# Six PSUM banks in turn and twelve pairs of weight buffers in the output stage of a hybrid decoder layer

## Chip, cores and metric

One NeuronCore of one Trainium2 chip runs the whole kernel. The metric is the device time of one execution in microseconds (us): the median of 3 runs before the change is 2421.57 us, the lowest 2419.29 and the highest 2424.53.

## What is computed

One decoder layer over 2048 tokens of width 1024, in float32, with 16 learned meta tokens in front. One input projection of 8712 columns feeds two branches: sliding-window attention (16 heads, 4 key heads, window 128, sinks) and an mLSTM (4 heads, chunked). Then the two branches are projected, merged and projected again:

```python
def _hybrid_mixer(u, w_in, ...):
    proj = u @ w_in
    (a_q, a_k, a_v, a_z, m_qk, m_v, m_i, m_f, m_o, m_z, g_a, g_m) = jnp.split(proj, SPLIT_POINTS, axis=-1)
    att = _swa_sink_branch(...)
    y_a = (att * jax.nn.silu(a_z)) @ w_attn_out
    cell = _mlstm_cell(...)
    hm = _head_layernorm(o_gate * cell, head_norm)
    y_m = (hm * jax.nn.silu(m_z)) @ w_mlstm_out
    merged = jax.nn.sigmoid(g_a) * y_a + jax.nn.sigmoid(g_m) * y_m
    return merged @ w_out
...
    h = h + _rmsnorm(y, norm_post[layer])
```

The change touches the last lines: the three matrix products with `w_attn_out`, `w_mlstm_out` and `w_out`, each 1024 by 1024, over 2048 tokens.

## The kernel before

Every product of two float32 matrices is made of three products of split operands: each operand is written as a high part in the format float32r and a low part that holds the rest, and high by high, high by low and low by high are summed in one PSUM bank. A *pair* of weight buffers is a high tile (`whi`) and a low tile (`wlo`) of 128 by 512 numbers; a *unit* (`un`) is the same for the data.

The program has two stages. The **projection stage** runs over two halves of the tokens, and in each over 18 blocks of weight columns; the work of attention and mLSTM is cut into small steps that are slipped between the projection matmuls. It leaves the attention result, the mLSTM result and the gates in DRAM (`att_d`, `hm_d`, `gate_d`). The **output stage** (the loop over `s` that ends the kernel) runs over four passes of 512 tokens. A pass has three products of two weight blocks each: attention (call its blocks A0 and A1, `ph` 0, L929), mLSTM (B0 and B1, `ph` 1, L929) and the last projection (O0 and O1, L951). A block has four groups of 24 matmuls of 128x512; a group fills one PSUM bank, and VectorE (DVE) reads it out: L934 in A0 and A1, L936 and L937 in B0 and B1 (which also splits the merged tile into a unit, L889 on ScalarE (ACT) and L890 on DVE), and L959 or L967 in O0 and O1 after ACT has squared it (L956).

`load_w` (L163) brings a block of weights: eight tiles of raw weights by DMA on SyncE's queue (L175, three buffers in the output stage, and two more in the projection stage), each split by ACT (`whi`, L181) and DVE (`wlo`, L182). The pairs come from the pool `wp`; in the output stage the first two of a block's eight come from tiles of their own (`whi2`, `wlo2`, four of each), so that a block takes six pairs of `wp` there and eight in the projection stage.

The order of TensorE (PE) is the order of the program text (`manual_schedule`). The order of the other engines' instructions and of the DMA issues is made ahead of the run by the framework's scheduler, which takes the earliest in the program among those that it holds ready; the raw loads and the splits are moved ahead by the priorities `DMA_LEAD` and `SPLIT_LEAD` (30 and 2; 100 for the second block of all). Each engine then works through its list strictly in order. A tile that is asked of a pool waits until the oldest of the pool's buffers under that name has been read for the last time.

PSUM's eight banks belong to four pools: `ps_p` (2, name `pj`), `ps_s` (one tile of 2 banks), `ps_t` (2, `tr`) and `ps_a` (2, `acc`). In the output stage only the two of `ps_p` are used.

Of the kernel before, what the change touches and what calls it, by code (L numbers as in the profile page):

```python
# [9 lines left out]
F32 = mybir.dt.float32  # L10
# [13 lines left out]
SB = 512  # L24
# [66 lines left out]
def hybrid_layer(ctx: ExitStack, tc: tile.TileContext, x, xT, mx, mxT, gpre, w_all, w2, negs, cw, cb,  # L91
                 gbias, hnorm, gpost, rope, ident, sel, bmask, out):
    nc = tc.nc
# [3 lines left out]
    def pool(name, bufs=1, space=None, es=ctx):  # L97
        kw = {} if space is None else {"space": space}
        return es.enter_context(tc.tile_pool(name=name, bufs=bufs, **kw))
# [1 line left out]
    const = pool("const")  # L101
    dram = pool("dram", 1, DRAM)
    units = pool("units", 16)
    wp = pool("wp", 9)
    stage = pool("stage", 4)
    ps_p = pool("ps_p", 2, PSUM)
    ps_s = pool("ps_s", 1, PSUM)
    ps_t = pool("ps_t", 2, PSUM)
    ps_a = pool("ps_a", 2, PSUM)
# [4 lines left out]
    def f(t):  # L114
        return t.bitcast(F32)
# [89 lines left out]
    with ExitStack() as es1:  # L205
# [490 lines left out]
        def token_proj(us, o, wh, wl, w, ps=None):  # L696
            if ps is None:
                ps = ps_p.tile([128, SB], F32, name="pj")
            n = 0
            for k in range(KT):  # L700
                for a, ww in ((0, wh), (0, wl), (1, wh)):
                    T.matmul(ps[:, :w], lhsT=us[k][:, a, o:o + 128], rhs=ww[k][:, :w],  # L702
                             start=(n == 0), stop=(n == 3 * KT - 1))
                    n += 1
                    if n % SLOT == 0 and n < 3 * KT:
                        slot()
            return ps

        def feat_proj(us, i, wh, wl):
            ps = ps_p.tile([128, SB], F32, name="pj")  # L710
            n = 0
            for k in range(KT):
                for a, ww in ((0, wh), (1, wh), (0, wl)):
                    T.matmul(ps, lhsT=ww[k][:, 128 * i:128 * i + 128], rhs=us[k][:, a],  # L714
                             start=(n == 0), stop=(n == 3 * KT - 1))
                    n += 1
                    if n % SLOT == 0 and n < 3 * KT:
                        slot()
            return ps
# [32 lines left out]
        for c in range(NHALF):  # L752
# [7 lines left out]
            for pi, (kind, arg, cols) in enumerate(PLAN):  # L760
# [24 lines left out]
                if kind == "A":  # L785
                    chains = []
                    for i in range(HALF_BLOCKS):
                        rs = None
                        if c == 0 and arg == 0:
# [9 lines left out]
                            if i < 4:  # L799
                                ps = first_ps[i]  # L800
                            else:
                                ps = token_proj(u[1], (i % 4) * 128, wh, wl, w, first_ps[i] if i < 6 else None)
# [3 lines left out]
                        else:  # L806
                            ps = token_proj(u[i // 4], (i % 4) * 128, wh, wl, w)
# [34 lines left out]
                elif kind == "M":  # L842
                    for i in range(HALF_BLOCKS):
                        mrep = max_rows(c, i + nb - HALF_BLOCKS, arg)
                        ps = token_proj(u[i // 4], (i % 4) * 128, wh, wl, w)
# [6 lines left out]
                else:  # L852
# [9 lines left out]
                    for n, (i, s) in enumerate(order):  # L862
                        nm, ix = arg[i]
                        ps = feat_proj(u[s], i, wh, wl)
# [19 lines left out]
    gpost_t = p2.tile([128, D], F32, name="gpost", bufs=1)  # L884
    nc.sync.dma_start(out=gpost_t, in_=gpost.partition_broadcast(128))

    def split_unit(src):
        un = units.tile([128, 2, SB], R, name="un")
        S.copy(un[:, 0], src)  # L889
        tt(un[:, 1], src, f(un)[:, 0], ALU.subtract)  # L890
        return un

    for s in range(SEQ // SB):
        sl = slice(s * SB, (s + 1) * SB)
        part = [None] * KT
        mg = [None] * KT
        for ph, (src, zn, gn) in enumerate(((att_d, "az", "ga"), (hm_d, "mz", "gm"))):
            us = []
            with (tc.high_priority(offset=150) if s == 0 and ph == 0 else ExitStack()):
                for k in range(KT):  # L900
                    early = s == 0 and ph == 0
                    if early:
                        a = p2.tile([128, SB], F32, name=f"part{k}", bufs=1)
                    else:
                        a = stage.tile([128, SB], F32, name="xs")
                    nc.sync.dma_start(out=a, in_=src[k, :, sl])
                    if early:
                        if k % 2 == 0:
                            zz = p2.tile([128, D], F32, name="y", bufs=4)
                        z = zz[:, k % 2 * SB:(k % 2 + 1) * SB]  # L910
                    else:
                        z = p2.tile([128, SB], F32, name="zl", bufs=3)
                    nc.sync.dma_start(out=z, in_=gate_d[zn][k, :, sl])
                    if ph == 0:
                        tt(a, a, z, ALU.mult)
                    else:
                        stt(a, a, hn_t[:, k:k + 1], z, ALU.mult, ALU.mult)
                    us.append(split_unit(a))
            for nb_ in range(2):
                wh, wl = load_w(w2, (2 * ph + nb_) * D * SB, SB, p2)  # L920
                for i in range(4):
                    j = nb_ * 4 + i
                    th = p2.tile([128, SB], F32, name="tl", bufs=3)
                    nc.sync.dma_start(out=th, in_=gate_d[gn][j, :, sl])
                    ps = ps_p.tile([128, SB], F32, name="pj")
                    n = 0
                    for k in range(KT):
                        for a, ww in ((0, wh), (1, wh), (0, wl)):
                            T.matmul(ps, lhsT=ww[k][:, 128 * i:128 * i + 128], rhs=us[k][:, a],  # L929
                                     start=(n == 0), stop=(n == 3 * KT - 1))  # L930
                            n += 1
                    if ph == 0:
                        part[j] = p2.tile([128, SB], F32, name=f"part{j}", bufs=1)
                        stt(part[j], th, 1.0, ps, ALU.add, ALU.mult)  # L934
                    else:
                        stt(th, th, 1.0, ps, ALU.add, ALU.mult)  # L936
                        tt(part[j], part[j], th, ALU.add)  # L937
                        mg[j] = split_unit(part[j])
        w_o = load_w(w2, 4 * D * SB, SB, p2)
        ys, sss = [], []  # L940
        for i in range(4):
            ys.append(p2.tile([128, D], F32, name="y", bufs=4))
            sss.append(p2.tile([128, 4], F32, name="yss", bufs=4))
        for nb_ in range(2):
            wh, wl = w_o if nb_ == 0 else load_w(w2, 5 * D * SB, SB, p2)
            for i in range(4):
                ps = ps_p.tile([128, SB], F32, name="pj")
                n = 0
                for k in range(KT):
                    for a, ww in ((0, wh), (0, wl), (1, wh)):  # L950
                        T.matmul(ps, lhsT=mg[k][:, a, 128 * i:128 * i + 128], rhs=ww[k],  # L951
                                 start=(n == 0), stop=(n == 3 * KT - 1))
                        n += 1
                y, ss = ys[i], sss[i]
                jk = p2.tile([128, SB], BF, name="jk2", bufs=1)
                S.activation(jk, ps, AF.Square, accum_out=ss[:, nb_:nb_ + 1])  # L956
                cs = slice(nb_ * SB, (nb_ + 1) * SB)
                if nb_ == 0:
                    tt(y[:, cs], ps, gpost_t[:, cs], ALU.mult)  # L959
                    ts(ss[:, 2:3], ss[:, 0:1], 1.0 / D, 16.0 * EPS, ALU.mult, ALU.add)  # L960
                    continue
                r0 = s * SB + i * 128
                xr = p2.tile([128, D], F32, name="xr")
                nc.sync.dma_start(out=xr, in_=x[r0:r0 + 128, :])
                ts(ss[:, 2:3], ss[:, 1:2], 1.0 / D, ss[:, 2:3], ALU.mult, ALU.add)  # L965
                G.tensor_tensor(ss[:, 3:4], ss[:, 2:3], mh_t[:, 0:1], ALU.pow)  # L966
                tt(y[:, cs], ps, gpost_t[:, cs], ALU.mult)  # L967
                for j in range(2):
                    cs = slice(j * SB, (j + 1) * SB)
                    stt(y[:, cs], y[:, cs], ss[:, 3:4], xr[:, cs], ALU.mult, ALU.add)  # L970
                    nc.sync.dma_start(out=out[r0:r0 + 128, cs], in_=y[:, cs])
# [54 lines left out]
```

## Time and profile before

| | |
|---|---|
| median of 3 runs | 2421.57 us |
| the profiled execution | 2425.9 us, its span 2424.2 us |
| PE busy with matmuls | 2377.3 us (98% of the span) |
| DVE, ACT, POOL busy | 1404.7, 1014.7, 558.6 us |
| projection stage, to about 1871.9 us | 1871.9 us |
| output stage, to the last matmul at 2418.2 us | 546.3 us |
| after the last matmul | 6.0 us |

The span is the time from the first to the last instruction of the trace; the execution's own time is 1.7 us longer. Busy time of PE counts a matmul from its start to its modelled end, and matmuls overlap, so a busy PE can still be a slow one: the count of matmuls in a stretch tells more. The granted clock (PEclk) is 1.00 where TensorE has its full 2.4 GHz and 0.5 where it has 1.2 GHz. POOL is GpSimd, SP is SyncE, and SPq its DMA issues.

### The profile page before, as it was taken

Reading aid. Unit: us, or ns where it says so; the run is one execution under the profiler, and the core shown is the slowest. Engines: PE = TensorE matmul, PEld = TensorE weight load, DVE = VectorE, ACT = ScalarE, POOL = GpSimd, SP = SyncE. Lnnn points to the kernel's source line nnn. Section 1 sums busy time; section 2 is a strip of 40 time slices with the busy share of each in tenths; the row PEclk is TensorE's granted clock in tenths of the full one; section 3 lists DMA queues with packets and bytes.
Section 4 is the critical chain, followed back from the end, with each engine's and each line's share of the span. In section 5 each row is a group of like instructions: output and inputs, shape, how many; then the busy total and the mean of one; then the engine's idle time right before and its main releaser. Section 6 shows DMA issues by size and latency. Waiting matters only on the chain.

```text
span 2424.2 us, 34730 instructions
## 1 busy us (share of the span) xinstructions
PE 2377.3 (98%) x11725; PEld 2017.7 (83%) x11725; DVE 1404.7 (58%) x3309; ACT 1014.7 (42%) x2674; POOL 558.6 (23%) x1151
## 2 busy tenths in 40 slices
PE   7999999999999999999999999999999999999999
PEld 7788988988898888888988888898888777878787
DVE  7776376366637633676367457637623565665654
ACT  6454354355435423454345345435423243333432
POOL 5332333223233310332323232233310000000000
PEclk9999999999999999999999999999999999999999
DMA  5113212231311234112212212221227767575752
GB/s 188 51 49 96 92 56 67 70 101 44 97 56 56 89 103 143 48 59 70 90 58 63 72 47 65 74 86 58 70 85 237 230 191 254 175 254 168 236 176 89
DMA packets 176162, 261.38 MB, mean 108 GB/s; under 512 B 18684, under 2 KB 68176, under 8 KB 175984
## 3 DMA queue, kind: packets, MB, share of 16 engines
q1 hardware_dynamic: 175984, 259.17, 33.7%
q8 instruction: 92, 1.51, 0.3%
q14 instruction: 86, 0.70, 0.1%
HBM read 200.35 MB, written 58.76 MB: 107 GB/s over the span
## 4 chain that ended last, share of the span: by engine, by line
PE 82%; DMA 6%; DVE 6%; ACT 3%; issue 2%; POOL 1%; SPq 0%; DVEq 0%; POOLq 0%; ACTq 0%
PE pj L714 35%; PE pj L702 22%; PE pj L929 10%; PE pj L951 3%; PE acc L479 3%; DMA wraw<-in_w 3%; PE s L427 3%; DVE wlo L182 2%; PE acc L546 2%; ACT whi L181 1%; PE tr L452 1%; DMA xs<-att_d 1%; DMA zl<-mz_d 1%; PE tr L400 1%; PE tr L546 1%
## 5 line engine op out<-in xcount | busy, mean ns | idle before, releaser
L714 PE MATMUL pj<-un,whi 128*128 128x512 f32 x2560 | 805.1, 396 | 0.0
L702 PE MATMUL pj<-whi,un 128*128 128x512 f32 (+2 forms) x1952 | 604.1, 371 | 0.0
L714 PEld LDWEIGHTS pj<-un,whi 128*128 128x128 f32 x2560 | 467.3, 188 | 88.4
L714 PE MATMUL pj<-un,wlo 128*128 128x512 f32 x1280 | 501.8, 392 | 0.0
L182 DVE TENSOR_TENSOR wlo<-wraw,whi 128x512 fp32r<-128x512 f32 (+2 forms) x480 | 325.5, 702 | 175.4 <-ACT whi L181 172.5
L702 PEld LDWEIGHTS pj<-whi,un 128*128 128x128 f32 x1952 | 361.3, 188 | 37.7 <-issue 1.3
L181 ACT CAST whi<-wraw 128x512 fp32r<-128x512 f32 (+2 forms) x480 | 283.0, 606 | 229.1 <-DMA wraw<-in_w 135.1
L702 PE MATMUL pj<-wlo,un 128*128 128x512 f32 (+2 forms) x976 | 355.9, 365 | 0.0
L929 PE MATMUL pj<-un,whi 128*128 128x512 f32 x1024 | 315.6, 389 | 5.4 <-DVE part L934 5.2
L714 PEld LDWEIGHTS pj<-un,wlo 128*128 128x128 f32 x1280 | 240.8, 188 | 53.3
L929 PEld LDWEIGHTS pj<-un,whi 128*128 128x128 f32 x1024 | 191.9, 188 | 46.6 <-issue 3.2
L929 PE MATMUL pj<-un,wlo 128*128 128x512 f32 x512 | 199.2, 389 | 0.0
L702 PEld LDWEIGHTS pj<-wlo,un 128*128 128x128 f32 x976 | 184.1, 189 | 14.7
L951 PE MATMUL pj<-whi,un 128*128 128x512 f32 x512 | 164.3, 400 | 8.8 <-DVE y L967 8.2
L727 ACT ACTIVATE xs<-pj 128x512 f32<-128x512 f32 x128 | 76.5, 598 | 209.6 <-PE pj L714 200.2
L436 ACT ACTIVATE P<-s,mn 128x144 f32<-128x144 f32 x256 | 95.1, 376 | 152.5 <-DVE mn L434 150.5
L966 POOL TENSOR_TENSOR yss<-yss,mhalf 128x1 f32<-128x1 f32 x16 | 8.8, 549 | 621.3 <-DVE yss L965 621.3
L445 POOL TENSOR_TENSOR Pm<-P,mn 128x64 f32<-128x64 f32 x64 | 38.0, 594 | 443.8 <-DVE mn L441 351.4
L951 PEld LDWEIGHTS pj<-whi,un 128*128 128x128 f32 x512 | 98.8, 193 | 32.0 <-DVE y L967 9.4
L462 POOL TENSOR_SCALAR_AFFINE_SELECT pp<-pc 128x512 fp32r<-128x512 f32 x120 | 84.5, 704 | 175.7 <-ACT pc L457 164.0
L929 PEld LDWEIGHTS pj<-un,wlo 128*128 128x128 f32 x512 | 96.1, 188 | 20.1
L951 PE MATMUL pj<-wlo,un 128*128 128x512 f32 x256 | 101.8, 398 | 0.5 <-DVE wlo L182 0.5
(330 smaller groups left out, 3320.2 us busy)
## 6 DMA issues: line engine op xcount, KB each, us to landing
wraw<-in_w_all SPq DMA_DIRECT2D x224, 256.0 KB, 3.3
wraw<-in_w SPq DMA_DIRECT2D x192, 256.0 KB, 3.4
wraw<-in_w_all SPq DMA_DIRECT2D x48, 192.0 KB, 2.5
ga_d<-xs SPq DMA_DIRECT2D x32, 256.0 KB, 2.4
att_d<-ao SPq DMA_DIRECT2D x64, 128.0 KB, 1.8
hm_d<-tho SPq DMA_DIRECT2D x64, 128.0 KB, 1.8
az_d<-xs SPq DMA_DIRECT2D x32, 256.0 KB, 2.4
mz_d<-xs SPq DMA_DIRECT2D x32, 256.0 KB, 2.4
```

The lines of the kernel that those rows point to most:

```text
L181: S.copy(hi[:, :w], raw[:, :w])
L182: tt(lo[:, :w], raw[:, :w], f(hi)[:, :w], ALU.subtract)
L427: T.matmul(sp[:, pa, c0:272], lhsT=qs[:, pr, pa, :], rhs=ks[:, i, c0:272], start=(i == 0), stop=(i == 1))
L436: S.activation(P[:, 2 * pa + pr], sp[:, pa, 128:272], AF.Exp, bias=mn[:, 2 * pr + pa:2 * pr + pa + 1], scale=-1.0, accum_out=mn[:, 4 + 2 * ...
L462: G.affine_select(pp[:, i], f(pc)[:, i], pattern=[[0, 4], [-1, 128]], compare_op=ALU.is_gt, fill=0.0, base=0, channel_multiplier=1)
L479: T.matmul(acc, lhsT=l, rhs=r.rearrange("p s q -> p (s q)"), start=(i == 0), stop=(i == len(ops) - 1))
L546: T.matmul(out, lhsT=l[:, a], rhs=r[:, b_], start=(start and n == 0), stop=(stop and n == 2))
L702: T.matmul(ps[:, :w], lhsT=us[k][:, a, o:o + 128], rhs=ww[k][:, :w], start=(n == 0), stop=(n == 3 * KT - 1))
L714: T.matmul(ps, lhsT=ww[k][:, 128 * i:128 * i + 128], rhs=us[k][:, a], start=(n == 0), stop=(n == 3 * KT - 1))
L727: S.activation(th, ps, AF.Tanh, scale=0.5)
L929: T.matmul(ps, lhsT=ww[k][:, 128 * i:128 * i + 128], rhs=us[k][:, a], start=(n == 0), stop=(n == 3 * KT - 1))
L951: T.matmul(ps, lhsT=mg[k][:, a, 128 * i:128 * i + 128], rhs=ww[k], start=(n == 0), stop=(n == 3 * KT - 1))
```

## The change

`wp` gets 12 buffers under each name instead of 9. A helper `bank()` hands out the PSUM tiles of the output stage from `ps_p`, `ps_t` and `ps_a` in turn, so six banks in place of two. The space for three more pairs (2 tiles of 2 KB for each of them, 12 KB per partition) is taken from the scratch that the program reserves for dynamic DMAs, which is set to 2048 bytes.

```diff
-    wp = pool("wp", 9)
+    wp = pool("wp", 12)
...
+    turn = [0]
+
+    def bank():
+        pl, nm = ((ps_p, "pj"), (ps_t, "tr"), (ps_a, "acc"))[turn[0] % 3]
+        turn[0] += 1
+        return pl.tile([128, SB], F32, name=nm)
...
                     nc.sync.dma_start(out=th, in_=gate_d[gn][j, :, sl])
-                    ps = ps_p.tile([128, SB], F32, name="pj")
+                    ps = bank()
...
             for i in range(4):
-                ps = ps_p.tile([128, SB], F32, name="pj")
+                ps = bank()
...
-    nc = bacc.Bacc("TRN2", target_bir_lowering=False, num_devices=1)
+    nc = bacc.Bacc("TRN2", target_bir_lowering=False, num_devices=1, dynamic_dma_scratch_size=2048)
```

## Rows read from the trace of the kernel before

**Rows 1.** Two stretches: length, busy by engine (instructions), clock, DMA share, GB/s.

```profile
0.00:1871.90 1871.90, 1845.79 (x9421) 1581.88 (x9421) 1082.45 (x2787) 829.80 (x2335) 549.80 (x1135) 1.00 0.26 81
1871.90:2418.20 546.30, 531.56 (x2306) 435.79 (x2304) 320.03 (x518) 184.23 (x337) 8.23 (x15) 0.99 0.63 199
```

**Rows 2.** The four output passes, PE alone: length, busy (matmuls), clock, DMA, GB/s.

```profile
1871.90:2008.65 136.75, 129.64 (x556) 0.98 0.69 217
2008.65:2151.10 142.45, 138.29 (x601) 0.99 0.67 212
2151.10:2287.57 136.47, 133.07 (x577) 0.99 0.68 215
2287.57:2418.25 130.68, 130.56 (x576) 1.00 0.47 149
```

**Rows 3.** Chain that ended last: start, length, work; instructions merged.

```profile
1793.40 73.47 PE pj L714 x324
...
2287.57 87.04 PE pj L929 x384
2374.61 43.53 PE pj L951 x192
```

**Rows 4.** What PE waited for over the span: us in total, times, longest.

```profile
PE tr L609 <- DVE ks L409: 9.4, 8, 1.5
PE pj L951 <- DVE y L967: 8.2, 3, 3.6
...
PE pj L929 <- DVE part L934: 5.2, 3, 2.8
```

**Rows 5.** Timeline of PE, two of the stalls: start, length, work, idle before.

```profile
1918.63 0.70 PE L929 MATMUL pj<-un,whi 128*128 128x512 f32 x2 [2.83 <-DVE part L934]
...
2000.01 0.79 PE L951 MATMUL pj<-whi,un 128*128 128x512 f32 x1 [3.58 <-DVE y L967]
```

**Rows 6.** Timeline of DVE, ACT and SP's issues before the stall at 2000 us.

```profile
1987.46 0.75 DVE L917 SCALAR_TENSOR_TENSOR xs<-xs,hn,zl 128x512 f32<-128x512 f32 x1 [3.08 <-DMA zl<-mz_d]
1993.35 2.00 DVE L182 TENSOR_TENSOR wlo<-wraw,whi 128x512 fp32r<-128x512 f32 x3 [2.67 <-ACT whi L181]
1999.28 0.68 DVE L967 TENSOR_TENSOR y<-pj,gpost 128x512 f32<-128x512 f32 x1
...
1981.38 1.98 ACT L181 CAST whi<-wraw 128x512 fp32r<-128x512 f32 x3 [1.29 <-PE pj L951]
...
1988.84 10.75 SPq L175 DMA_DIRECT2D wraw<-in_w  x8
```

**Rows 7.** Stretches right after two stalls: length, busy by engine, clock, DMA, GB/s.

```profile
2000.01:2005.80 5.79, 5.79 (x14) 4.53 (x15) 3.55 (x6) 0.00 (x0) 0.58 (x2) 0.51 0.85 281
...
2274.76:2279.00 4.24, 4.24 (x12) 3.34 (x13) 3.55 (x6) 0.00 (x0) 0.59 (x2) 0.60 0.88 301
```

**Rows 8.** DMA issues, the output stage's weight loads: count, size, us to landing.

```profile
wraw<-in_w SPq DMA_DIRECT2D x192, 256.0 KB, 3.4
```

**Rows 9.** Timeline of DVE where B1 ends and O0 begins, third pass.

```profile
2239.21 0.69 DVE L936 SCALAR_TENSOR_TENSOR tl<-tl,pj 128x512 f32<-128x512 f32 x1 [0.84 <-PE pj L929]
...
2241.84 0.69 DVE L182 TENSOR_TENSOR wlo<-wraw,whi 128x512 fp32r<-128x512 f32 x1 [0.61 <-ACT whi L181]
2242.45 0.69 DVE L890 TENSOR_TENSOR un<-part,un 128x512 fp32r<-128x512 f32 x1
```

**Rows 10.** Timeline of DVE at one block boundary of the projection stage.

```profile
1727.88 0.77 DVE L182 TENSOR_TENSOR wlo<-wraw,whi 128x512 fp32r<-128x512 f32 x1
```

**Rows 11.** Timeline of POOL, DVE and PE near the program's start.

```profile
49.06 0.39 POOL L253 TENSOR_TENSOR qkv<-ropa,ropb 128x96 f32<-128x96 f32 x1
...
51.28 2.70 POOL L253 TENSOR_TENSOR qkv<-ropa,ropb 128x96 f32<-128x96 f32 x1
...
51.25 2.48 DVE L182 TENSOR_TENSOR wlo<-wraw,whi 128x512 fp32r<-128x512 f32 x4
...
55.47 0.28 PE L371 MATMUL tr<-ident,xs 16*128 16x16 f32 x1 [4.88 <-POOL xs L253]
```

## The prediction

> **What bounds the kernel now.** I read the busy times by stretch first. PE is busy for 1845.79 of 1871.9 us in the projection stage and 531.56 of 546.3 us in the output stage, while DVE has 320 us and ACT 184 us of work there and the DMA engines a share of 0.63 [rows 1]. So PE is the bound, and only its idle or slow time can be gained. The output stage by passes is the second view: 136.75, 142.45 and 136.47 us, and 130.68 us for the last [rows 2]. The cuts of the first two passes lie some matmuls beside the true borders (556 and 601 matmuls instead of 576), so I use their sum. The last pass is the measure of an unhindered one: 576 matmuls in 87.04 + 43.53 = 130.57 us, 0.2267 us each, in one unbroken run at full clock [rows 3]. Four of these are 522.3 us. The stage takes 546.3, so 24.0 us are lost in the first three passes.
>
> The waits of PE say where: 8.2 us of L951 for the read-out of a bank by L967, 5.2 us of L929 for the read-out by L934, each in three stalls [rows 4]. PE's idle time in the stage is 546.3 - 531.56 = 14.7 us in all [rows 1], so shorter stalls add 1.3. The rest of the loss, 9.3 us, is slow time behind the stalls. After the stall at 2000 us PE has a granted clock of 0.51 (the level of 1.2 GHz) for 5.79 us, with 14 matmuls where 25 would fit (5.79 / 0.2267); after that at 2274.76 us it has 0.60, with 12 instead of 18 or 19 [rows 7]. That is 2.6 and 1.5 us; the restart of the pipeline after each stall makes the rest.
>
> Then the timeline of one stall. PE stops for 3.58 us until 2000.01 [rows 5], because only two banks exist and L967, which empties the one that it needs, ends at 1999.96 [rows 6]. L967 has little work but stands in DVE's list behind splits: DVE waits 3.08 us for a gate tile (L917, 1987.46) and 2.67 us for a high part (L182, 1993.35), and these wait for DMA. Further back, three splits of O1 wait on ACT until PE frees pairs (1981.38), the low parts free the raw buffers late, and SP issues the next eight weight loads only from 1988.84 on, over 10.75 us [rows 6]. The bank was full when its group ended, 3.58 us of stall and one group of 24 x 0.2267 = 5.44 us before 2000.0, so at 1991.0; it was emptied 9.0 us later. With two banks a group finds its bank free only if the read-out takes less than 5.44 us.
>
> **Part by part.** *Six banks.* A bank is wanted again five groups after it is full, 5 x 5.44 = 27.2 us, against a worst lateness of 9.0 us (for the stall of 2.83 us [rows 5] by the same count 8.3 us). So all waits on read-outs go, with 18 us to spare. No instruction is added. The banks of `ps_t` and `ps_a` are idle by then: from 1793.40 on PE does nothing but L714 into `pj` for 324 matmuls and 73.47 us [rows 3]. What is late next is data: weights, units, and merged tiles.
>
> *Twelve pairs.* A block of the output stage takes six of them, so twelve hold two whole blocks; with nine, three of O1's six splits waited for O0's last group (1981.38 in rows 6). Splits that were made just in time get a block's time, 4 x 5.44 = 21.8 us, as slack. The number of loads and splits stays: 192 loads of 3.4 us to landing in this stage [rows 8]. The DMA engines, at a share of 0.67 to 0.69 in the first three passes [rows 2], move the same bytes in less time: the share rises by 24 in 416, to 0.72. DVE has 320 us of work for 522.
>
> *What I leave in place.* The tightest spot that the change doesn't widen is where B1 ends. The last merged tile must become a unit before PE needs it in O0's first group, 21 matmuls or 4.76 us after B1's end at about 2239.2. It was done at 2243.14 [rows 9], 0.8 us ahead, with two splits in between, one of which let DVE idle for 0.61 us. I charge one split of 0.69 us more there in each of four passes: 2.8 us. So 24.0 - 2.8 = 21.2 us of the stage go. Bounds: 24.0, and what the first rival below leaves.
>
> *Projection stage.* Here twelve pairs let four splits of the next block run early instead of one. PE never waits there for weights but in the first 20 us. The eight stalls at L609 (9.4 us together, at most 1.5 each) end with DVE's L409 [rows 4]; in the one near 1729 us a split of 0.77 us stands just ahead of L409 on DVE [rows 10]. The spare pairs take the first splits out of the burst, but PE frees the first four pairs of the old block at that moment for the last four of the new one, so four may still stand there. I take 0, between a gain of 9.4 us and a loss that the second rival prices. At the start, one POOL instruction took 2.70 us beside four splits on DVE, and 0.39 us two microseconds earlier without them, and PE waited 4.88 us for what POOL did next [rows 11]. More splits may come together there, or leave earlier: from -4.9 to +4.9 us, and I take 0. The Trainium skill (SBUF — State Buffer, Who interferes with whom) says that a DVE instruction with two SBUF inputs shuts out a GpSimd instruction that reads SBUF for its whole length; the row of 2.70 us agrees. By that rule alone splits moved over POOL's work only trade places with those taken from the burst, and the sum stays the same.
>
> *Scratch.* The rows of DMA issues all name SP's queue, as that of the weight loads does [rows 8]; none names POOL. I cost the smaller scratch at nothing. Were it used, the time to landing of the weight loads, now 3.4 us, would show it.
>
> *Sum.* The profiled execution took 2425.9 us. Minus 21.2 is 2404.7. It is 0.18% above the median of the runs, so 2404.7 x 2421.57 / 2425.9 = 2400.4 us.
>
> **Rivals.** *A new wait takes half back.* PE now runs ahead of DVE, which still idles on DMA for 2 to 3 us at a time [rows 6]. If such a wait falls between L937 and L890 at the end of B1, the unit is late by 2.67 - 0.8 = 1.9 us to 3.08 - 0.8 = 2.3 us, with 1.5 to 2.6 us of slow clock behind it [rows 7]: 3.4 to 4.9 us in three passes, 10 to 15 us. For it: the idle 0.61 us in that very spot [rows 9]. Against it: earlier splits leave fewer loads late. It gives 2408 to 2415 us.
>
> *The projection stage pays.* 36 blocks have their splits moved. If a split of 0.70 us comes in front of an instruction of attention or mLSTM on whose result PE waits, as at L609 [rows 4, 10], once in each block, that is 25 us, more than the 21.2 gained: about 2425 to 2435 us. It decides from 0.6 us per block on. Against it: steps of attention and mLSTM come earlier in the program than the next block's splits, and PE waits there for 26 us in all (1871.9 - 1845.79) [rows 1].
>
> *It does nothing.* If DVE's and the DMAs' pace and not the banks held the first three passes, PE would meet the same delay as missing data: 2417 to 2426 us. Against it: DVE is busy for 59% of the stage, and in long runs between the stalls PE runs at 0.2267 us per matmul.
>
> *Banks in turn.* The Trainium skill (TensorE: Matmul & The Clock Gate, A second HAM failure mode: psum-queue depth-cycling) describes a kernel whose clock fell back because its matmuls cycled through banks. Here the last pass changes its bank every 24 matmuls and keeps a clock of 1.00 [rows 2, 3], which speaks against it. As a mechanism of this kernel: a slow stretch like that at 2000 us, 2.6 us lost [rows 7], once in each turn of six banks, 16 times, is 42 us; with the 21.2 gained about 2440 us.
>
> **How the numbers follow.** Forecast (2389 to 2406 us) 0.63; half taken back (2406 to 2415) 0.22; nothing 0.07; the projection stage pays 0.06; banks in turn 0.02. A measurement of this kernel can tell about 0.2%, 4.8 us. Faster is 0.63 + 0.22 = 0.85, the same 0.07, slower 0.08. The range goes from 2389, with all 24 us gained and most of L609's 9.4, to 2414, where the first rival nearly ends; somewhat over 0.8 of the chance lies in it. The time is that of the forecast, 2400.4.
>
> **What would show it.** In the profile after, no wait of PE for L934, L936, L959 or L967; the three first passes at 131 to 132 us each, at a clock of 1.00; read-outs still up to 9 us late on DVE, but without a stall; ACT's splits no longer released by PE in O0. If PE waits for `un` at L951, the first rival is right; if the time up to the output stage's first matmul, 1871.9 us, grows by more than 5 us, the second. I would be wrong altogether if the first three passes stay at 136 us and more with PE waiting for weights or units.

## The result, and the profile after

The changed kernel takes 2398.98 us (median of 4 runs, 2396.55 to 2401.19), against 2420.6 us for the kernel before, run beside it: a ratio of 0.9908 [0.9891, 0.9925], so 22 us or 0.9% faster. The forecast was 2400.4 us. The line of busy times on the page of after has PE busy for 99% of the span instead of 98%:

```profile
PE 2369.8 (99%) x11725; PEld 2016.4 (84%) x11725; DVE 1401.1 (58%) x3309; ACT 1012.2 (42%) x2674; POOL 562.2 (23%) x1151
```

The four output passes of after, PE alone (length, busy time and matmuls, granted clock, DMA share, GB/s), the answer to [rows 2]:

```profile
1870.40:2001.10 130.70, 130.70 (x578) 1.00 0.73 226
2001.10:2131.70 130.60, 130.60 (x577) 1.00 0.71 227
2131.70:2262.30 130.60, 130.60 (x578) 1.00 0.71 223
2262.30:2393.00 130.70, 130.70 (x578) 1.00 0.46 148
```

All four now look like the last one of before: PE has no gap, the clock is 1.00 throughout, and the DMA share of the first three rose from 0.67 to 0.69 up to 0.71 to 0.73. The list of PE's waits in after (total us, times, longest), against [rows 4]:

```profile
PE tr L609 <- DVE ks L409: 6.6, 5, 1.5
PE tr L371 <- POOL xs L253: 6.4, 4, 5.8
PE tr L515 <- DVE rawm L517: 3.8, 4, 2.6
```

No line of the output stage is left in it, and L609, which belongs to the projection stage, lost three of its eight stalls. (From `bank()` on the line numbers are 7 higher: the matmuls of `ph` 0 and 1 are L936, of the last product L958, the read-outs L941, L943, L966 and L974.)

Where PE stands at the two borders is read from the first start of a line (name, count, durations, then "first to last start"). In before the projection's first L427 starts at 78.0 and the first output matmul at 1872.1; in after:

```profile
L427 PE MATMUL s<-ks,qs x512: 229/287/392, 79.5 to 1775.8; 128*128 128x272 f32 x160, 128*128 128x144 f32 x11
L936 PE MATMUL pj<-un,whi x384: 389/389/389, 1870.2 to 2349.0; 128*128 128x512 f32 x192
```

So the span of the profiled executions went from 2424.2 to 2399.2 us, 25.0 us, in three parts: the output stage from 546.0 to 522.9 us (23.1 gained; counted here from the first output matmul to the end of the last), the stretch between the two borders from 1794.1 to 1790.7 us (3.4 gained), and the start 1.5 us longer.

All kernels of this study, each with its own median, and with the same two lengths from the same views:

| kernel | banks | pairs | median us | L427 to output | output stage |
|---|---|---|---|---|---|
| before | 2 | 9 | 2421.57 | 1794.1 | 546.0 |
| smaller scratch alone | 2 | 9 | 2420.44 | 1794.3 | 538.6 |
| twelve pairs alone | 2 | 12 | 2412.13 | 1790.5 | 538.7 |
| six banks alone | 6 | 9 | 2404.22 | 1794.5 | 523.5 |
| ten pairs, more of the stage's own | 6 | 10 | 2405.07 | 1794.8 | 528.9 |
| a turn of three places | 4 | 12 | 2398.95 | 1790.4 | 522.8 |
| first trial at L371 | 6 | 12 | 2398.57 | 1789.9 | 522.8 |
| second trial at L371 | 6 | 12 | 2398.73 | 1791.3 | 523.0 |
| after | 6 | 12 | 2398.98 | 1790.7 | 522.9 |

### The profile page after: what moved, and what is told of

It is laid out like the page before. It is cut to its first block, busy times and chain, and to the rows that moved or that the text cites. A ratio compares the mean times of both kernels' runs of the same rounds, so it can differ in the third digit from the quotient of the medians.

```text
span 2399.2 us, 34747 instructions
## 1 busy us (share of the span) xinstructions
PE 2369.8 (99%) x11725; PEld 2016.4 (84%) x11725; DVE 1401.1 (58%) x3309; ACT 1012.2 (42%) x2674; POOL 562.2 (23%) x1151
## 4 chain that ended last, share of the span: by engine, by line
PE 93%; DVE 3%; ACT 1%; POOL 1%; issue 1%; DMA 0%; SPq 0%; DVEq 0%; POOLq 0%; ACTq 0%
PE pj L714 36%; PE pj L702 23%; PE pj L936 5%; PE tr L936 5%; PE acc L936 5%; PE acc L479 3%; PE tr L958 3%; PE acc L958 3%; PE s L427 3%; PE pj L958 2%; PE acc L546 2%; PE tr L452 1%; PE tr L400 1%; PE tr L546 1%; DVE wlo L182 1%
## 5 line engine op out<-in xcount | busy, mean ns | idle before, releaser
L714 PE MATMUL pj<-un,whi 128*128 128x512 f32 x2560 | 803.7, 395 | 0.0
L714 PEld LDWEIGHTS pj<-un,whi 128*128 128x128 f32 x2560 | 466.6, 188 | 88.1
L714 PE MATMUL pj<-un,wlo 128*128 128x512 f32 x1280 | 501.2, 392 | 0.0
L702 PEld LDWEIGHTS pj<-whi,un 128*128 128x128 f32 x1952 | 361.3, 188 | 37.8 <-issue 1.3
L714 PEld LDWEIGHTS pj<-un,wlo 128*128 128x128 f32 x1280 | 240.3, 188 | 53.0
L936 PE MATMUL pj<-un,whi 128*128 128x512 f32 x384 | 118.3, 389 | 0.0
L936 PE MATMUL tr<-un,whi 128*128 128x512 f32 x320 | 98.6, 389 | 0.0
L936 PE MATMUL acc<-un,whi 128*128 128x512 f32 x320 | 98.6, 389 | 0.0
L484 DVE TENSOR_TENSOR ao<-acc,xs 64x256 f32<-64x256 f32 x64 | 26.7, 417 | 109.9 <-ACT xs L481 108.3
L381 ACT COPY qkv<-pj 128x320 f32<-128x320 f32 x112 | 30.3, 322 | 140.6 <-PE pj L702 140.6
L490 DVE SCALAR_TENSOR_TENSOR xs<-raw,cw,xs 128x512 f32<-128x512 f32 x96 | 71.9, 748 | 28.6 <-ACT xs L501 17.6
```

## The experiments

### Six banks alone

The kernel before with `bank()`, nine pairs, and the scratch as it was. In the two traces every engine runs the same instructions in the same order; only the banks differ.

```diff
+        pl, nm = ((ps_p, "pj"), (ps_t, "tr"), (ps_a, "acc"))[turn[0] % 3]
...
-                    ps = ps_p.tile([128, SB], F32, name="pj")
+                    ps = bank()
```

> Six banks in turn, but nine pairs of weight buffers and the scratch as before. If the wait for read-outs carries most of the gain and the pairs the rest: no wait of PE for a read-out, the projection stage ends at 1871.9 us as before, and PE meets some late splits where a new pass begins, 2 to 4 us in each of three passes; the output stage takes 528 to 535 us and the whole 2403 to 2411 us. If the pairs do nothing for the output stage: 522 to 524 us there and 2398 to 2402 us in all. If the pace of DVE and the DMAs held the passes and not the banks: 2417 us and more.

Measured: 2404.22 us (2402.66 to 2405.14), ratio 0.9926 [0.9909, 0.9943]. PE's waits, of which the last two are all that the output stage has, and the projection's L609 as before:

```profile
PE tr L609 <- DVE ks L409: 9.4, 8, 1.5
...
PE acc L958 <- DVE wlo L182: 0.3, 1, 0.3
PE tr L936 <- DVE wlo L182: 0.2, 1, 0.2
```

The banks alone bring the output stage from 546.0 to 523.5 us: 22.5 of the 24.0 us lost. The total fell where it was expected, but not for the reason given: a remainder of 5 to 12 us was expected in the output stage for want of pairs, and it is 0.5 us of waits. The 5 us by which this kernel is behind after stand mostly in the projection stage.

### Twelve pairs alone

The kernel before with the twelve pairs and the smaller scratch, two banks. Every engine runs the same instructions in the same order as in after; against before, the order on DVE and ACT differs.

```diff
-    wp = pool("wp", 9)
+    wp = pool("wp", 12)
```

> Twelve pairs and the small scratch, but two banks as before. In the changed kernel 27 of the 96 read-outs end more than 5.44 us (one group) after their group, against 11 before; with two banks each of these is a stall. If the banks carry the gain: the output stage takes 540 to 560 us, with PE waiting for L934, L959 or L967, and the whole 2415 to 2435 us. If late splits were the cause of the late read-outs and the pairs cure them: 525 to 530 us and 2400 to 2407 us.

Measured: 2412.13 us (2411.21 to 2414.45), ratio 0.9962 [0.9947, 0.9977]. In the output stage PE still waits for read-outs, 9.2 us instead of 14.2 us:

```profile
PE tr L609 <- DVE ks L409: 6.1, 4, 1.5
PE pj L929 <- DVE part L934: 4.6, 4, 1.9
PE pj L951 <- DVE yss L960: 4.2, 3, 2.3
...
PE pj L951 <- DVE y L967: 0.4, 1, 0.4
```

The time lies below the 2415 to 2435 us expected for a gain that the banks carry. The pairs alone are worth more than that, 9.7 us of the median (2421.83 us for the kernel before beside these runs): 3.6 us in the projection stage, where four L609 stalls instead of eight are left, and by subtraction some 6 us in the output stage. That last part is not shown by one profile: the smaller-scratch kernel below, with nine pairs, happened to have an output stage of 538.6 us too. With the banks there, the 6 us are no longer to be had; the two gains overlap (17.6 us for the banks and 9.7 us for the pairs alone, against 22.8 us for both, all three counted from 2421.83).

### The smaller scratch alone

```diff
-    nc = bacc.Bacc("TRN2", target_bir_lowering=False, num_devices=1)
+    nc = bacc.Bacc("TRN2", target_bir_lowering=False, num_devices=1, dynamic_dma_scratch_size=2048)
```

> The kernel before with the smaller scratch alone (2048 bytes reserved for dynamic DMAs), nine pairs and two banks; the order of the instructions is that of the kernel before on every engine. My theory, that the scratch costs nothing: within 0.2% of the kernel before (about 2417 to 2426 us), the weight loads of the output stage still 3.4 us to landing, the output stage 544 to 548 us, and PE still waits about 9.4 us at L609. Rival, that the scratch is used by the transfers: a landing time well over 3.4 us, and slower than before. Second rival, that the 4 us found in the projection stage with twelve pairs come from the scratch and not from the pairs: this kernel would have its first output matmul 4 us earlier after the projection's first matmul (1790 instead of 1794 us).

Measured: 2420.44 us (2417.33 to 2425.01), ratio 0.9994 [0.9981, 1.0007]. The output stage's weight loads (size, us from issue to landing) and L609:

```profile
wraw<-in_w SPq DMA_DIRECT2D x192, 256.0 KB, 3.4
...
PE tr L609 <- DVE ks L409: 9.4, 8, 1.5
```

Both stand as before, and the stretch from L427 to the output takes 1794.3 us. So the scratch costs and gains nothing that these runs can tell, and the 4 us of the projection stage come from the pairs. One expectation missed: the output stage took 538.6 us in this profile, not 544 to 548. The order of the instructions is that of before on every engine, so with two banks the stalls differ from execution to execution; the 17 runs of the kernel before beside this one reach from 2415.64 to 2431.28 us, the four of after from 2396.55 to 2401.19.

### A turn of three places

After, with a turn of three places. The third place hands out the two buffers of `ps_t` by turns, so the stage uses four banks: one of `ps_p` is wanted again two groups after it is full, one of `ps_t` five groups after.

```diff
-        pl, nm = ((ps_p, "pj"), (ps_t, "tr"), (ps_a, "acc"))[turn[0] % 3]
+        pl, nm = ((ps_p, "pj"), (ps_p, "pj"), (ps_t, "tr"))[turn[0] % 3]
```

> The changed kernel, but the read-outs go through three places in turn: the two banks of ps_p, then a bank of ps_t. A bank is wanted again at the earliest two groups, 10.88 us, after it is full. The worst read-out of the changed kernel ends 8.2 us after its group. If only that lateness counts: no wait of PE in the output stage, 522 to 524 us there, and the time of the changed kernel within 2 us (2397 to 2401 us). If more banks are needed than the count of lateness says, because lateness adds up when PE runs ahead: waits for read-outs come back, 2403 us and more.

Measured: 2398.95 us (2398.19 to 2401.3), ratio 0.9908 [0.9893, 0.9923], the same as after. The first three passes, in the columns used above:

```profile
1868.00:1998.70 130.70, 130.70 (x577) 1.00 0.71 223
1998.70:2129.40 130.70, 130.70 (x578) 1.00 0.72 228
2129.40:2260.10 130.70, 130.70 (x578) 1.00 0.70 225
```

So the count that the prediction made is enough for the read-outs of this execution, the latest of which ends 7.8 us after its group. Where a read-out ends up to 9.0 us after its group, the bank must be wanted again after more than that: one group (5.44 us) is too little, two (10.88 us), which two of three groups have here, are enough. A ring of exactly three banks was not run. The slack of six banks is not always idle: in the execution with ten pairs below, four read-outs end 10.9 to 13.2 us after their group, more than 10.88, and PE doesn't wait for any of them.

### Ten pairs in the projection stage

After, with ten pairs in `wp` and three of a block's eight pairs from tiles of the output stage's own: sixteen pairs in the output stage as in after, ten in the projection stage.

```diff
-    wp = pool("wp", 12)
+    wp = pool("wp", 10)
...
-            own = p2 is not None and k < 2
-            hi = p2.tile([128, SB], R, name="whi2", bufs=4) if own else wp.tile([128, SB], R, name="whi")
-            lo = p2.tile([128, SB], R, name="wlo2", bufs=4) if own else wp.tile([128, SB], R, name="wlo")
+            own = p2 is not None and k < 3
+            hi = p2.tile([128, SB], R, name="whi2", bufs=6) if own else wp.tile([128, SB], R, name="whi")
+            lo = p2.tile([128, SB], R, name="wlo2", bufs=6) if own else wp.tile([128, SB], R, name="wlo")
```

> The kernel after with ten pairs instead of twelve for both stages, and six pairs of the output stage's own (three of each block's eight, instead of two): the output stage has sixteen pairs as in the kernel after, the projection stage has ten. If the projection stage's 4 us (three stalls at L609 that are gone) need twelve pairs, PE waits there 8 to 9.4 us at L609 and the projection takes 1793 to 1795 us, the whole 2402 to 2404 us; if one pair more is enough, 6.6 us, 1790 to 1791 us, and 2398 to 2400 us. The output stage has no wait of PE for a read-out in either case: 522.5 to 523.5 us.

Measured: 2405.07 us (2404.22 to 2411.01), ratio 0.9932 [0.9909, 0.9954]. In the projection stage the first theory holds: ten pairs are not enough (1794.8 us, all eight stalls there); the whole is 1 us over the 2402 to 2404 us that it gave. In the output stage the expectation missed, and what came is the first rival of the prediction. PE's waits, then DVE and ACT in the first pass, where B1 ends and O0 begins (start, length, work, idle before and what ended it):

```profile
PE tr L609 <- DVE ks L409: 10.2, 8, 1.5
...
PE tr L958 <- ACT un L896: 4.2, 1, 4.2
```

```profile
1967.12 0.69 DVE L182 TENSOR_TENSOR wlo<-wraw,whi 128x512 fp32r<-128x512 f32 x1 [2.56 <-ACT whi L181]
1967.73 0.68 DVE L943 SCALAR_TENSOR_TENSOR tl<-tl,pj 128x512 f32<-128x512 f32 x1
...
1968.93 0.68 DVE L944 TENSOR_TENSOR part<-part,tl 128x512 f32<-128x512 f32 x1
...
1966.47 1.97 ACT L181 CAST whi<-wraw 128x512 fp32r<-128x512 f32 x3 [3.14 <-DMA wraw<-in_w]
1969.64 0.62 ACT L896 CAST un<-part 128x512 fp32r<-128x512 f32 x1 [1.21 <-DVE part L944]
```

The last group of B1 was full at 1961.3, but its read-out L943 stands on DVE behind a split, that split behind ACT's high part, and that behind a weight load that landed late. The unit's high part came at 1970.26, and PE, which had run 21 matmuls into O0, waited 4.22 us for it. The pass then took 136.6 us instead of 130.7, 5.9 us, of which 1.7 are more than the wait. By the times it is an event of one execution: the profiled one took 2411.01 us, the other three 2404.22 to 2405.59.

### The wait at L371: the order of POOL's work

At the start PE waits for POOL's work on the meta tokens (L371 on L253), 4.88 us in before [rows 11] and 5.78 us in after, where a run of five splits stands on DVE ahead of L242 and of the two small copies (L366, L367) that POOL waits for. The first trial put four of them behind the copies.

```diff
+                with (tc.issue_after(mdone[0].ins) if lead == 100 and k > 0 else ExitStack()):
+                    tt(lo[:, :w], raw[:, :w], f(hi)[:, :w], ALU.subtract)
...
-            V.tensor_copy(kv[:, 0:64], kv[:, 64:128])
+            mdone.append(V.tensor_copy(kv[:, 0:64], kv[:, 64:128]))
```

> The changed kernel, but near the start four low-part splits of the second weight block are kept behind the meta tokens' DVE work (L242 to L367), which they came to precede. In the changed kernel PE waits 5.78 us at L371 and 2.56 us at L515, against 4.88 and 1.60 before. If the early splits delay that chain: L371's wait falls to 3 us or less, and the whole to 2394 to 2397 us. If POOL beside the splits is what matters (its instruction of 2.70 us before): POOL is slowed by the same splits a little later, the wait stays at 4.5 us or more, and the time within 1 us of the changed kernel's.

Measured: 2398.57 us (2396.35 to 2399.3), ratio 0.9903 [0.9888, 0.9918], no different from after. DVE's five splits, POOL's next instruction and PE's wait:

```profile
50.82 3.08 DVE L182 TENSOR_TENSOR wlo<-wraw,whi 128x512 fp32r<-128x512 f32 x5
...
51.03 2.97 POOL L250 TENSOR_TENSOR ropa<-xs,rope 16x32 f32<-16x32 f32 x1 [0.90 <-DVE xs L367]
53.98 0.21 POOL L251 TENSOR_TENSOR ropb<-xs,rope 16x16 f32<-16x16 f32 x1
...
54.74 0.28 PE L371 MATMUL tr<-ident,xs 16*128 16x16 f32 x1 [5.73 <-POOL xs L253]
```

POOL could start earlier and then hung in one small instruction for 2.97 us, for as long as the run of splits lasted; the wait at L371 stayed. The Trainium skill (SBUF — State Buffer, Who interferes with whom) says that a DVE instruction with two SBUF inputs contends with a GpSimd instruction that reads SBUF, and that the lock on the port they share is exclusive. The trace agrees, and here the shut-out lasts for five such instructions that follow each other without a gap.

The second trial put the four splits behind the last DVE step of the meta tokens' keys (L374) instead.

```diff
-            tt(KM[g][:, 1], tr[:, 0:NM], f(KM[g])[:, 0], ALU.subtract)
+            mdone.append(tt(KM[g][:, 1], tr[:, 0:NM], f(KM[g])[:, 0], ALU.subtract))
```

> The kernel after, in which four early low-part splits of the second weight block (DVE, five in one run beside the meta tokens' work on POOL) are kept behind the last DVE step of the meta tokens' keys (L374). If a run of splits on DVE shuts out POOL, the POOL instructions of L250 to L253 take 0.2 to 0.6 us each there instead of up to 2.97, PE's wait at L371 falls from 5.8 us to 3 us or less, and the time is 2394 to 2397 us, provided the block's first matmuls don't wait for the splits. If the wait at L371 is set by something else, or comes back as a wait for weights, the time is within 1.5 us of that of the kernel after (2399 us).

Measured: 2398.73 us (2397.02 to 2399.89), ratio 0.99 [0.9881, 0.9919], again the same as after. POOL, PE and DVE near the start:

```profile
52.57 0.24 POOL L250 TENSOR_TENSOR ropa<-xs,rope 16x32 f32<-16x32 f32 x1 [0.90 <-DVE xs L367]
...
53.54 0.23 PE L371 MATMUL tr<-ident,xs 16*128 16x16 f32 x1 [2.96 <-POOL xs L253]
...
54.43 3.41 DVE L182 TENSOR_TENSOR wlo<-wraw,whi 128x512 fp32r<-128x512 f32 x5
...
69.66 0.23 PE L515 MATMUL tr<-ident,xs 16*128 16x16 f32 x1 [2.07 <-DVE xs L242]
```

The instruction of 2.97 us takes 0.24 us, and the wait at L371 falls from 5.73 us in the first trial (5.78 in after) to 2.96 us: that the splits held POOL is shown. But little of the time was gained: from L227, ahead of all this, to the first L427 it is 35.4 us, against 35.7 to 36.3 us in the three kernels with twelve pairs and an untouched start. At 69.66 PE waits 2.07 us for DVE's L242, which it does not do in after; that DVE was late there because it did the splits while PE ran ahead is likely, but was not varied. The expectation of 2394 to 2397 us was wrong: most of a wait taken away came back 16 us later at another line.

## Why the prediction was right, and where not

*What bounds the stage* was right. 24.0 us were said to be lost in the output stage, to waits for banks and to the slow clock behind them, and 23.1 us are gained. The clock is 1.00 in all passes: the stretches at 0.51 and 0.60 [rows 7] went with the stalls, as the sum supposed. Of the 9.3 us behind the stalls, more was clock than the prediction counted. It missed a third slow stretch in before, behind the stall that ends at 2138.31 (0.59 over 4.19 us). The groups behind the three stalls take 8.26, 7.18 and 7.20 us instead of 5.44, 6.3 us together, where it had 4.1 for two stalls and left the rest to restarts.

*Six banks remove all waits on read-outs*: shown, with the banks alone. What was to make it visible, late read-outs without a stall, is there. In after, the last matmul of the fourth group of an O1 block and its read-out:

```profile
1984.48 0.39 PE L958 MATMUL acc<-whi,un 128*128 128x512 f32 x1
...
1991.85 0.68 DVE L974 TENSOR_TENSOR y<-acc,gpost 128x512 f32<-128x512 f32 x1
```

The bank is full at 1984.87 and empty at 1992.53, 7.7 us later, and PE goes on without a gap. Counted over the 96 groups of the trace, 23 read-outs of after end more than 5.44 us after their group (11 in before; the 27 in the expectation for twelve pairs was too many), the latest 8.2 us. DVE has not become faster; its lateness lost its effect.

*Twelve pairs* were put in the wrong stage. The prediction gave them the output stage, where O1's splits waited for O0 [rows 6], and took the projection stage as 0. The wait in O0 did go: L951 releases five of ACT's splits in before (6.7 us), L958 none in after. But it moved: L929 releases six in before (28.0 us) and L936 fourteen in after (46.8 us). With six banks the pairs add 0.6 us in the output stage (523.5 to 522.9), and 3.8 us in the projection stage (1794.5 to 1790.7). The step that failed is the one that said of L609's stalls that four splits may still stand in front of L409. That holds in the second half, where four stalls of 1.5 us remain. In the first half three of the four are gone, and the fourth, at which the splits ahead are still of 512 columns, grew from 0.20 to 0.51 us. Counted from the first L427, the lead of after over before grows at just these three places, to 0.9 us near 194 us, 2.4 near 407 and 3.8 near 618, and falls to 3.4 at the fourth. DVE in the first half ahead of the stall at 405.00, in before:

```profile
399.23 1.72 DVE L182 TENSOR_TENSOR wlo<-wraw,whi 128x512 fp32r<-128x512 f32 x2
...
402.23 0.77 DVE L182 TENSOR_TENSOR wlo<-wraw,whi 128x384 fp32r<-128x384 f32 x1
...
404.23 0.42 DVE L599 SCALAR_TENSOR_TENSOR tho<-tho,acc 128x256 f32<-128x256 f32 x1
404.57 0.28 DVE L409 TENSOR_TENSOR ks<-tr,ks 128x128 fp32r<-128x128 f32 x1
```

and at the same place in after:

```profile
399.43 1.02 DVE L182 TENSOR_TENSOR wlo<-wraw,whi 128x384 fp32r<-128x384 f32 x2
...
401.73 0.56 DVE L182 TENSOR_TENSOR wlo<-wraw,whi 128x384 fp32r<-128x384 f32 x1
...
403.52 0.29 DVE L409 TENSOR_TENSOR ks<-tr,ks 128x128 fp32r<-128x128 f32 x1
403.73 0.41 DVE L599 SCALAR_TENSOR_TENSOR tho<-tho,acc 128x256 f32<-128x256 f32 x1
```

With twelve pairs the splits in front of L409 are the short ones of a block of 384 columns, since the last ones of the 512-column block ahead of it were made earlier, and L409 stands ahead of L599. It is done 1.04 us sooner, about what PE waited there (1.07 us). The order of L409 and L599 is the scheduler's choice; it was not varied by itself, so how much of the gain it makes is not shown. The gain lies inside the bound of 9.4 us that the prediction kept.

*The tight spot at the end of B1* was priced at a split of 0.69 us in each pass, 2.8 us. The spot was the right one, the price too high. The first group of O0 in the chain of after (start, length, work) takes slightly more than 5.44 us in three passes:

```profile
1957.45 5.64 PE tr L958 x24
2088.23 5.59 PE tr L958 x24
2218.98 5.54 PE tr L958 x24
```

That is 0.20 + 0.15 + 0.10 = 0.45 us. The margin was also read too small. The unit's high part (ACT) is wanted after 21 matmuls, but its low part (DVE) only by the 24th, which in before starts at 2244.22: 1.1 us after 2243.14, not 0.8. In after it is just used up; in the first pass DVE waits there, as the first rival had it, 2.79 us for a high part, and the last unit is done at 1962.53, where the 24th matmul starts at 1962.59:

```profile
1958.66 0.69 DVE L182 TENSOR_TENSOR wlo<-wraw,whi 128x512 fp32r<-128x512 f32 x1 [2.79 <-ACT whi L181]
1959.27 0.68 DVE L943 SCALAR_TENSOR_TENSOR tl<-tl,pj 128x512 f32<-128x512 f32 x1
...
1961.84 0.69 DVE L897 TENSOR_TENSOR un<-part,un 128x512 fp32r<-128x512 f32 x1
```

*The rivals.* The first, a new wait that takes half back, is real but rare: it is the 4.22 us of one execution with ten pairs, 5.9 us with what follows, where the prediction had 3.4 to 4.9 us in a pass. In after it costs 0.2 us at most in a pass: in the first, more than half of DVE's 2.79 us lie before the last group of B1 is full (1957.5). The second, that the projection stage pays, is refuted: it gained. The third, that data and not banks held the passes, is refuted by the banks alone. The fourth had a rule of the Trainium skill beside it (TensorE: Matmul & The Clock Gate, A second HAM failure mode: psum-queue depth-cycling); with six banks in turn the clock is 1.00 in every pass, so nothing of the sort is seen here.

*The sum.* 21.2 us were forecast for the profiled execution. Measured: 23.1 in the output stage, 3.4 in the projection stage, 1.5 lost at the start, and 0.3 less gained outside the span, 24.7. The misses are 1.9 us too little in the output stage, for the price at the end of B1, and 3.4 us in the projection stage, taken as 0; the start hid part of them. The start was taken as 0 within 4.9 us, and its 1.5 us are not the pairs'. They are there already at the wait at L227 (43.15 us, in before 41.62), ahead of L371; from there to the first L427 both kernels take 36.3 to 36.4 us. Between 20 and 30 us the granted clock was 0.83 in before and 0.72 in after. It was 0.68 with six banks alone, whose order is that of before and whose first L427 comes at 79.4, and 0.83 with the pairs alone and with the turn of three places, which start as after does and have theirs at 77.2 and 77.6. Why the clock differs at the start is open. That the forecast lies only 1.4 us from the median of after, where the profiled gain is 3.5 us off, is partly luck: the profiled execution of before lay 4.3 us above its median, that of after 2.2.

## What to carry to other kernels

To size a ring of PSUM banks, measure in the trace how long after a group's last matmul its read-out ends, at worst, and divide by the time of a group: here 9.0 by 5.44 us asks for two more banks beside the one that is being filled, and six banks were no faster than a turn in which two groups out of three get just that (2398.98 and 2398.95 us). Take the worst of several executions and leave a bank to spare: one execution here had a read-out 13.2 us late. A late read-out need not be made earlier if a bank that lies idle can stand in for it, and here the slow clock behind the stalls went with them. Where a change has two parts, price each in every stage that it touches: the pairs paid in a stage that the change was not about, and a wait taken away at one line (L371) can come back at another, here 16 us later.

## What the runs showed of the hardware

A POOL instruction of 0.24 us took 2.97 us beside five splits on DVE that followed each other without a gap, each with two SBUF inputs; moved out of their way it took 0.24 us again. It isn't so beside every such run: in after, beside the five splits that start at 51.77 us, three POOL instructions in a row took 0.72 to 0.73 us each (0.29 to 0.39 just before), so none was held for the whole run. What decides between the two is not shown. And the stalls of the output stage with two banks were not the same from execution to execution (546.0 and 538.6 us with an identical order of instructions), and the spread is narrower without them: 15.6 us over 17 runs of the kernel before, 5.0 us over the 18 runs of after, of the turn of three places and of the two trials at L371.
